# Shifting the preparation of state-space weights between GpSimd, VectorE and ScalarE in a two-layer diffusion block

## The chip, the cores and the metric

One core of a Trainium2 chip runs the whole block in one launch. The metric is the device time of one execution in microseconds; of three executions of the kernel before the median is 1510.47.

## The reference, cut to what matters

Two layers share one residual stream: 512 latent tokens and 256 context tokens of width 1024. Layer 0 is windowed grouped-query attention (16 query heads of 128, a sink logit for each head), layer 1 a bidirectional S5 state space with 128 groups of 16 channels and 64 complex states each. Every branch is gated by silu(z) and followed by an output projection and a layer norm.

```python
abar = jnp.exp(lam * dt)                                  # discretise
bbar = ((abar - 1.0) / lam)[..., None] * bmat
...
bu = jnp.einsum('btgn,gpn->btgp', u_blk, bbar)            # scan
hs = linear recurrence of bu with abar
y = jnp.einsum('btgp,gnp->btgn', hs, cmat).real
...
x = layer_norm(alpha * x + gate * ((y * jax.nn.silu(z)) @ w_out[i]), ln_g[i], ln_b[i])
```

## The kernel before, in words

The sequence is cut into steps of 8 tokens, so that the S5 layer becomes matmuls with weights that depend on the parameters alone: 64 **in-state weights** (powers of abar times B, from tokens to state), 32 **out-state weights** (C times the powers 0 to 8 of abar, from state to tokens), and a lag kernel made from them on TensorE. These weights are made on the chip while layer 0 runs, because layer 0 loads TensorE heavily and GpSimd (POOL in the profile) has little else to do. They are stored in DRAM scratch and read back in layer 1.

- `gen_w` makes one in-state weight with four tensor_tensor operations of 128x512 and 128x256 (L885 to L888), all on POOL. `w_tiles` gives it its buffers: the first EW=8, made by `early` during the first head's projections, borrow the attention's buffers `pth`, `ptl` and `zs`; the rest, made by `bg` in attention steps 1 to 21 (NW=22), have a pool of their own (`gE`, `gB`, `gm`, `gW`).
- `gen_o` makes one out-state weight: three small operations (L919 to L921) and, for each of two directions, two products and a sum over nine powers (L931 to L933, 128x576). `DO`, `DP`, `DQ` send numbers 3, 7 and 11 to VectorE (DVE), all others to POOL. Its `lag` part is 16 small matmuls (L948), two ScalarE (ACT) copies and two DVE additions, queued one weight later. QA=27 out-state weights belong to the attention from step 22 on, the other 5 to the output projection of layer 0, in its first NB=3 side steps, with buffers (`go2`) that lie where the attention's (`go`) lay.
- `layer0` runs 48 attention steps (8 head pairs by 6 blocks of 128 queries): `att_s` computes scores and softmax, `att_o` transposes the probabilities, splits them into a high and a low part (`pth`, `ptl`) and multiplies with V. Projections of the next pair ("dense" pieces) are interleaved.
- `outproj0` multiplies by the output weights, block by block of 128 tokens; `norm` computes mean and rstd (the rstd by three Newton steps on 128x1 operands, L293 and L294, and L285 ahead of them), L631 normalizes, `make_h1` transposes (L1013), scales (four tiles on DVE at L1018, four on ACT at L1020) and splits the result for layer 1, whose projection (`pul`, `puc`) follows.

All matmuls are done three times with high and low parts (`mm3`, L155 to L157). Each engine works through its instructions in order. The order on every engine comes from a planner that simulates the program with its own costs; `high_priority` with a negative offset puts the weight making behind the rest. All DMAs of the weights go through the one queue of SyncE (SP).

Of the kernel before, what the change touches and what calls it, by code (L numbers as in the profile page):

```python
# [111 lines left out]
F32 = mybir.dt.float32  # L112
# [21 lines left out]
class K:  # L134
# [141 lines left out]
    def norm(self, rs, pool):  # L276
# [14 lines left out]
        for i in range(3):  # L291
            t, yn = nt[:, 2 * i:2 * i + 1], nt[:, 2 * i + 1:2 * i + 2]
            nc.vector.scalar_tensor_tensor(t, y, xe[:, i:i + 1], y, op0=ALU.mult, op1=ALU.mult)  # L293
            nc.vector.scalar_tensor_tensor(yn, t, -3.0, y, op0=ALU.add, op1=ALU.mult)  # L294
            y = yn
# [35 lines left out]
def layer0(k, bg, early, late):  # L331
# [92 lines left out]
    def att_s(p, q, kk, qb):  # L424
# [26 lines left out]
        hs = slice(2 * p, 2 * p + 2)  # L451
        if not lat:
            nc.vector.tensor_reduce(mc, Sc, axis=AX.X, op=ALU.max)
            nc.vector.scalar_tensor_tensor(nm, mc, -SCALE, k.nsink[:, hs], op0=ALU.mult, op1=ALU.min)
# [9 lines left out]
        nc.vector.tensor_add(es, es, sm)  # L464
# [175 lines left out]
DW, DO, DP, DQ = 100, 4, 100, 14  # L640
# [215 lines left out]
def w_tiles(k, pool):  # L856
# [7 lines left out]
    z = k.qp.tile([128, 2, 768], F32, name="zs", bufs=2).rearrange("p h q -> p (h q)")  # L864
    return eb + [z[:, 512 * i:512 * i + 512].rearrange("p (d r a q) -> p d r a q", d=2, r=2, a=2) for i in range(3)]


def gen_w(k, tiles, i):
# [15 lines left out]
    tt = nc.gpsimd.tensor_tensor  # L884
# [7 lines left out]
def open_o(k, pool, q0, q1, gob):  # L892
# [3 lines left out]
    k.nc.sync.dma_start(k.dd, k.a["dd"][:, 16 * q0:16 * q1])  # L896


def gen_o(k, pool, q):

    nc, a = k.nc, k.a
    n = DO if q < DQ else DP
    eng = nc.vector if q % n == n - 1 else nc.gpsimd
# [18 lines left out]
    for d in range(2):  # L922
# [3 lines left out]
        def cc(t):  # L926
            return cb[:, t, d][:, :, None].to_broadcast([128, 4, 9, 16])

        def pb(o_):
            return pp[:, d, o_:o_ + 36].rearrange("p (g k) -> p g k", g=4)[:, :, :, None].to_broadcast([128, 4, 9, 16])  # L930
        eng.tensor_tensor(o, cc(0), pb(0), op=ALU.mult)  # L931
        eng.tensor_tensor(x, cc(1), pb(36), op=ALU.mult)  # L932
        last = eng.tensor_tensor(o, o, x, op=ALU.add)  # L933
# [70 lines left out]
def make_h1(k, b, n):  # L1004
# [4 lines left out]
    for j in range(2):  # L1009
# [4 lines left out]
        for i in range(4):  # L1014
            kk = 4 * j + i
            g, c = k.h1g[:, r, kk:kk + 1], k.h1b[:, r, kk:kk + 1]
            if j == 0:
                nc.vector.tensor_scalar(hf[:, kk], t[:, i], g, c, op0=ALU.mult, op1=ALU.add)  # L1018
            else:
                nc.scalar.activation(hf[:, kk], t[:, i], AF.Identity, bias=c, scale=g)  # L1020
# [312 lines left out]
N0, NW, EW = 1, 22, 8  # L1333
QO, QN = 32, 1
QA, NB = 27, 3
# [7 lines left out]
def main(tc, a):  # L1343
# [4 lines left out]
    k.wprio = 300  # L1348
    k.nw = NW
# [8 lines left out]
    with contextlib.ExitStack() as es:  # L1358
# [16 lines left out]
        with contextlib.ExitStack() as e2:  # L1375
# [51 lines left out]
            def gens(upto, pool):  # L1427
                nonlocal nw
                while nw < upto:
                    with tc.high_priority(offset=-GP):  # L1430
                        gen_w(k, w_tiles(k, pool), nw)
# [158 lines left out]
```

## Time and profile before

| | |
|---|---|
| median of three executions | 1510.47 us (1504.64 to 1512.83) |
| the profiled execution | 1508.56 us, its span 1506.8 us |
| TensorE busy | 1404.2 us (93%) |
| VectorE busy | 1040.2 us (69%) |
| ScalarE busy | 645.8 us (43%) |
| GpSimd busy | 635.0 us (42%) |
| mean granted TensorE clock | 0.971 of full speed |

The span runs from the first to the last instruction of the profiled execution; 1.8 us lie around it. The attention lasts from about 165 to 668 us, the output projection of layer 0 to about 870 us, layer 1 to the end. Times of rows are microseconds from the span's start.

### The profile page before, as it was taken

Reading aid. Unit: us, or ns where it says so; the run is one execution under the profiler, and the core shown is the slowest. Engines: PE = TensorE matmul, PEld = TensorE weight load, DVE = VectorE, ACT = ScalarE, POOL = GpSimd, SP = SyncE. Lnnn points to the kernel's source line nnn. Section 1 sums busy time; section 2 is a strip of 40 time slices with the busy share of each in tenths; the row PEclk is TensorE's granted clock in tenths of the full one; section 3 lists DMA queues with packets and bytes.
Section 4 is the critical chain, followed back from the end, with each engine's and each line's share of the span. In section 5 each row is a group of like instructions: output and inputs, shape, how many; then the busy total and the mean of one; then the engine's idle time right before and its main releaser. Section 6 shows DMA issues by size and latency. Waiting matters only on the chain.

```text
span 1506.8 us, 25662 instructions
## 1 busy us (share of the span) xinstructions
PE 1404.2 (93%) x9092; PEld 1134.5 (75%) x9092; DVE 1040.2 (69%) x2711; ACT 645.8 (43%) x1256; POOL 635.0 (42%) x542
## 2 busy tenths in 40 slices
PE   7999999999997899987988799999999999999997
PEld 2554789988886788875766688888777777888886
DVE  7734748777684477876759922789887896565376
ACT  1310546555464446552333234445556545343220
POOL 0004469999998676988975800000000000000240
PEclk9999999999998899998999899999999999999999
DMA  9876566766664446488795476667666796655541
GB/s 335 274 232 203 163 192 202 225 214 208 200 221 152 131 146 200 141 248 265 214 280 158 137 257 226 210 210 231 220 226 220 223 292 213 197 195 168 180 152 60
DMA packets 252639, 309.57 MB, mean 205 GB/s; under 512 B 45408, under 2 KB 151648, under 8 KB 252512
## 3 DMA queue, kind: packets, MB, share of 16 engines
q1 hardware_dynamic: 227168, 295.36, 61.5%
q10 hardware_dynamic: 25344, 12.59, 2.9%
q8 instruction: 71, 1.16, 0.3%
q14 instruction: 56, 0.46, 0.1%
HBM read 239.20 MB, written 77.07 MB: 210 GB/s over the span
## 4 chain that ended last, share of the span: by engine, by line
PE 54%; POOL 13%; DVE 13%; DMA 10%; issue 5%; ACT 3%; SPq 1%; POOLq 0%; DVEq 0%; ACTq 0%
PE pg L155 4%; PE pg L157 4%; PE pg L156 4%; PE adaps L166 3%; PE po L156 3%; PE po L157 3%; PE po L155 3%; DMA wsc<-gW 3%; PE ins L1084 3%; POOL gm L885 3%; POOL gm L886 2%; PE pul L155 2%; PE pul L156 2%; PE pul L157 2%; POOL gW L888 2%
## 5 line engine op out<-in xcount | busy, mean ns | idle before, releaser
L1318 POOL TENSOR_TENSOR xt<-xt,lng 128x512 f32<-128x512 f32 (+1 forms) x9 | 13.7, 1532 | 584.5 <-DMA xt<-n0sc 584.5
L146 DVE TENSOR_TENSOR wl<-wr,wh 128x1024 fp32r<-128x1024 f32 x104 | 137.8, 1325 | 142.9 <-ACT wh L145 140.3
L145 ACT ACTIVATE wh<-wr 128x1024 fp32r<-128x1024 f32 x104 | 109.9, 1057 | 188.0 <-PE pc L156 52.0
L155 PE MATMUL pg<-ga,wh 128*128 128x512 f32 x256 | 100.3, 392 | 0.8 <-ACT ga L1243 0.8
L157 PE MATMUL pg<-ga,wl 128*128 128x512 f32 x256 | 100.5, 393 | 0.0
L933 POOL TENSOR_TENSOR gO<-gO,gX 128x576 f32<-128x576 f32 x58 | 94.9, 1635 | 4.4
L885 POOL TENSOR_TENSOR gm<-gB,gE 128x512 f32<-128x512 f32 x56 | 78.6, 1403 | 23.6 <-DVE zs L500 19.3
L931 POOL TENSOR_TENSOR gO<-gcb,gpp 128x576 f32<-128x576 f32 x58 | 77.0, 1333 | 25.2 <-PE lag L948 20.6
L932 POOL TENSOR_TENSOR gX<-gcb,gpp 128x576 f32<-128x576 f32 x58 | 82.1, 1415 | 2.8
L886 POOL TENSOR_TENSOR gm<-gB,gE 128x512 f32<-128x512 f32 x56 | 82.6, 1475 | 0.0
L461 ACT ACTIVATE P<-P,nm 128x512 f32<-128x512 f32 (+1 forms) x64 | 49.7, 776 | 76.3 <-DVE nm L445 76.2
L487 DVE TENSOR_TENSOR ptl<-PT,pth 128x512 fp32r<-128x512 f32 (+1 forms) x96 | 60.9, 639 | 22.6 <-ACT pth L486 21.9
L1107 DVE TENSOR_TENSOR x<-m 128x64 f32<-128x64 f32 x376 | 74.7, 217 | 2.4
L146 DVE TENSOR_TENSOR gl<-gr,gh 128x512 fp32r<-128x512 f32 x48 | 50.2, 1047 | 31.2 <-ACT gh L145 31.2
L467 ACT ACTIVATE P<-P,es 128x512 f32<-128x512 f32 (+2 forms) x96 | 60.5, 682 | 19.7 <-DVE es L465 19.6
L155 PE MATMUL pq<-hh,wh 128*128 128x512 f32 x160 | 66.0, 413 | 2.8 <-ACT hh L255 2.8
L486 ACT ACTIVATE pth<-PT 128x512 fp32r<-128x512 f32 (+1 forms) x96 | 52.4, 559 | 34.4 <-PE PT L483 26.0
L483 PE MATMUL PT<-ident,P 128*128 128x128 f32 x352 | 61.3, 282 | 6.2 <-DVE vl L388 2.8
L155 PE MATMUL po<-woh,gh 128*128 128x512 f32 (+1 forms) x156 | 59.9, 394 | 7.5 <-ACT woh L580 4.7
L156 PE MATMUL pq<-hl,wh 128*128 128x512 f32 x160 | 65.8, 412 | 0.8 <-DVE hl L256 0.8
L157 PE MATMUL pq<-hh,wl 128*128 128x512 f32 x160 | 64.9, 406 | 0.3 <-DVE wl L146 0.3
L156 PE MATMUL po<-wol,gh 128*128 128x512 f32 (+1 forms) x156 | 61.7, 395 | 3.5 <-DVE wol L581 3.5
(317 smaller groups left out, 4673.2 us busy)
## 6 DMA issues: line engine op xcount, KB each, us to landing
wr<-w SPq DMA_DIRECT2D x40, 512.0 KB
osc<-gO SPq DMA_DIRECT2D x64, 256.0 KB
wr<-wout SPq DMA_DIRECT2D x32, 512.0 KB
W<-wsc SPq DMA_DIRECT2D x32, 512.0 KB
om<-osc SPq DMA_DIRECT2D x64, 256.0 KB
wr<-glu SPq DMA_DIRECT2D x32, 512.0 KB
gE<-esc SPq DMA_DIRECT2D x56, 256.0 KB
gB<-bt SPq DMA_DIRECT2D x56, 256.0 KB
```

Of the source, the lines that this page charges most:

```text
L145: nc.scalar.activation(hi, raw, AF.Copy)
L146: nc.vector.tensor_sub(lo, raw, f32(hi))
L155: mm(out, wh, mh, start=start, stop=False)
L156: mm(out, wh, ml, start=False, stop=False)
L157: mm(out, wl, mh, start=False, stop=stop)
L483: nc.tensor.transpose(T[:, j, h, :], P[h][:, c * 128:(c + 1) * 128], k.ident)
L885: tt(x(m1), x(B), eb(0), op=ALU.mult)
L886: tt(x(m2), x(B), eb(1), op=ALU.mult)
L931: eng.tensor_tensor(o, cc(0), pb(0), op=ALU.mult)
L932: eng.tensor_tensor(x, cc(1), pb(36), op=ALU.mult)
L933: last = eng.tensor_tensor(o, o, x, op=ALU.add)
L1107: nc.vector.tensor_add(x, m[:, :, 0], m[:, :, 1])
```

## The change

- `norm`: the six Newton operations become tensor_scalar with two per-partition scalars in place of scalar_tensor_tensor. In `att_s` the 128x2 operations `nm` (context blocks only) and `es` become two 128x1 tensor_scalar operations each.
- In-state weights: 12 in place of 8 are made early, the odd ones on DVE, with two fixed `zs` tiles that are used in turn; the rest are made in attention steps 1 to 19 (NW=20).
- Out-state weights: all on POOL; power 0 is a scaled copy on ACT (`k.sg`, a new small DMA at each opening), so that L931 to L933 work on 8 powers (128x512). 22 in place of 27 belong to the attention, from step 20 on, and 10 to five side steps of the output projection.
- `make_h1`: all eight scaled tiles on ACT.

```diff
-            nc.vector.scalar_tensor_tensor(t, y, xe[:, i:i + 1], y, op0=ALU.mult, op1=ALU.mult)
-            nc.vector.scalar_tensor_tensor(yn, t, -3.0, y, op0=ALU.add, op1=ALU.mult)
+            nc.vector.tensor_scalar(t, y, xe[:, i:i + 1], y, op0=ALU.mult, op1=ALU.mult)
+            nc.vector.tensor_scalar(yn, t, -3.0, y, op0=ALU.add, op1=ALU.mult)
...
-            nc.vector.scalar_tensor_tensor(nm, mc, -SCALE, k.nsink[:, hs], op0=ALU.mult, op1=ALU.min)
+            for h in range(2):
+                nc.vector.tensor_scalar(nm[:, h:h + 1], mc[:, h:h + 1], -SCALE, k.nsink[:, 2 * p + h:2 * p + h + 1],
+                                        op0=ALU.mult, op1=ALU.min)
...
-        nc.vector.tensor_add(es, es, sm)
+        for h in range(2):
+            nc.vector.tensor_scalar(es[:, h:h + 1], es[:, h:h + 1], sm[:, h:h + 1], None, op0=ALU.add)
...
+    if i < 2:
+        k.wz[i] = k.qp.tile([128, 2, 768], F32, name="zs", bufs=2).rearrange("p h q -> p (h q)")
+    z = k.wz[i % 2]
...
-    tt = nc.gpsimd.tensor_tensor
+    tt = eng.tensor_tensor
...
+    sg = pool.tile([128, 2], F32, name="sg")
+    k.nc.sync.dma_start(sg, k.a["sgn"])
+    k.sg = sg[:, 0:1]
...
-    n = DO if q < DQ else DP
-    eng = nc.vector if q % n == n - 1 else nc.gpsimd
+    eng = nc.gpsimd
...
-        eng.tensor_tensor(o, cc(0), pb(0), op=ALU.mult)
-        eng.tensor_tensor(x, cc(1), pb(36), op=ALU.mult)
-        last = eng.tensor_tensor(o, o, x, op=ALU.add)
+
+        nc.scalar.activation(o[:, :, 8 * d], cb[:, 0, d], AF.Copy, scale=k.sg)
+        o8, x8 = o[:, :, 1 - d:9 - d], x[:, :, 0:8]
+        eng.tensor_tensor(o8, cc(0), pb(0), op=ALU.mult)
+        eng.tensor_tensor(x8, cc(1), pb(36), op=ALU.mult)
+        last = eng.tensor_tensor(o8, o8, x8, op=ALU.add)
...
-            if j == 0:
-                nc.vector.tensor_scalar(hf[:, kk], t[:, i], g, c, op0=ALU.mult, op1=ALU.add)
-            else:
-                nc.scalar.activation(hf[:, kk], t[:, i], AF.Identity, bias=c, scale=g)
+            nc.scalar.activation(hf[:, kk], t[:, i], AF.Identity, bias=c, scale=g)
...
-N0, NW, EW = 1, 22, 8
+N0, NW, EW = 1, 20, 12
 QO, QN = 32, 1
-QA, NB = 27, 3
+QA, NB = 22, 5
...
-                        gen_w(k, w_tiles(k, pool), nw)
+                        gen_w(k, w_tiles(k, pool, nw), nw, nc.vector if pool is None and nw % 2 else nc.gpsimd)
```

## Rows read from the trace of the kernel before

**Rows 1.** The page: busy time, share of the span, instructions.
```profile
PE 1404.2 (93%) x9092; PEld 1134.5 (75%) x9092; DVE 1040.2 (69%) x2711; ACT 645.8 (43%) x1256; POOL 635.0 (42%) x542
```
**Rows 2.** Stretches: length, busy time by engine, clock, DMA share, GB/s.
```profile
470.00:510.00 40.00, 24.71 (x169) 21.37 (x168) 17.06 (x49) 15.10 (x36) 27.96 (x27) 0.81 0.50 156
800.00:870.00 70.00, 53.05 (x357) 45.34 (x359) 68.62 (x138) 22.09 (x47) 55.99 (x45) 0.88 0.45 144
```
**Rows 3.** Waits of TensorE from 420 to 560 us.
```profile
PE lag L948 <- POOL gO L933: 8.7, 1, 8.7
PE S L155 <- DVE nm L445: 5.8, 1, 5.8
```
**Rows 4.** Timeline of VectorE, 500 to 512 us.
```profile
503.42 0.29 DVE L919 TENSOR_TENSOR gX<-gcb,gpp 128x128 f32<-128x128 f32 x1 [6.26 <-POOL gO L933]
...
505.90 0.08 DVE L445 DVE_READ_ACCUMULATOR2_ANT nm<- 128x1 f32 x1
```
**Rows 5.** Timeline of TensorE, the matmul that follows.
```profile
506.04 0.58 PE L155 MATMUL S<-kh,qh 128*128 128x256 f32 x1 [5.77 <-DVE nm L445]
```
**Rows 6.** Timeline of GpSimd, first instructions of weights, last of one.
```profile
111.01 1.29 POOL L885 TENSOR_TENSOR zs<-ptl,pth 128x512 f32<-128x512 f32 x1 [71.14 <-DMA pth<-esc]
...
174.22 1.29 POOL L885 TENSOR_TENSOR zs<-ptl,pth 128x512 f32<-128x512 f32 x1 [10.88 <-DMA wsc<-zs]
...
201.29 1.29 POOL L885 TENSOR_TENSOR gm<-gB,gE 128x512 f32<-128x512 f32 x1 [19.32 <-DVE zs L500]
...
474.41 0.40 POOL L919 TENSOR_TENSOR gX<-gcb,gpp 128x128 f32<-128x128 f32 x1 [5.42 <-DMA gpp<-ppsc]
...
779.89 1.75 POOL L933 TENSOR_TENSOR gO<-gO,gX 128x576 f32<-128x576 f32 x1
805.58 0.87 POOL L919 TENSOR_TENSOR gX<-gcb,gpp 128x128 f32<-128x128 f32 x1 [23.93 <-DVE nt L294]
...
865.37 2.46 POOL L933 TENSOR_TENSOR gO<-gO,gX 128x576 f32<-128x576 f32 x1
```
**Rows 7.** Groups of GpSimd by form, whole span.
```profile
L933 POOL TENSOR_TENSOR gO<-gO,gX 128x576 f32<-128x576 f32 x58 | 94.9, 1635 | 4.4
...
L932 POOL TENSOR_TENSOR gX<-gcb,gpp 128x576 f32<-128x576 f32 x58 | 82.1, 1415 | 2.8
...
L931 POOL TENSOR_TENSOR gO<-gcb,gpp 128x576 f32<-128x576 f32 x58 | 77.0, 1333 | 25.2 <-PE lag L948 20.6 <-PE h1t L1013 4.4
```
**Rows 8.** Waits of GpSimd: total, times, longest.
```profile
POOL zs L885 <- DMA wsc<-zs: 35.5, 3, 18.0
...
POOL gO L931 <- PE lag L948: 20.6, 9, 9.8
POOL gX L919 <- DVE gO L933: 19.5, 3, 10.4
```
**Rows 9.** Groups of VectorE by form, 795 to 870 us.
```profile
L631 DVE TENSOR_SCALAR nrm<-R,mv,nt 128x512 f32<-128x512 f32 x11 | 10.4, 971 | 0.1
...
L1018 DVE TENSOR_SCALAR h1f<-h1t,h1g,h1b 128x128 f32<-128x128 f32 x24 | 8.2, 396 | 0.0
...
L293 DVE SCALAR_TENSOR_TENSOR nt<-nt,xe 128x1 f32<-128x1 f32 x12 | 6.3, 530 | 0.1
...
L294 DVE SCALAR_TENSOR_TENSOR nt<-nt 128x1 f32<-128x1 f32 x12 | 4.7, 390 | 0.1
```
**Rows 10.** The same lines on VectorE, 1440 to 1507 us.
```profile
L293 DVE SCALAR_TENSOR_TENSOR nt<-nt,xe 128x1 f32<-128x1 f32 x8 | 1.7, 218 | 0.2
...
L294 DVE SCALAR_TENSOR_TENSOR nt<-nt 128x1 f32<-128x1 f32 x8 | 1.3, 158 | 0.2
```
**Rows 11.** Line 288: duration in ns min/median/max, first and last start.
```profile
L288 DVE TENSOR_SCALAR ih<-ih x10: 97/153/155, 800.6 to 1500.7; 128x1 int32<-128x1 int32 x10
```
**Rows 12.** Waits of TensorE from 800 to 900 us.
```profile
PE h1t L1013 <- DVE nrm L631: 13.8, 5, 5.8
```
**Rows 13.** A group of ScalarE by form, 795 to 870 us.
```profile
L1020 ACT ACTIVATE h1f<-h1t,h1b,h1g 128x128 f32<-128x128 f32 x24 | 9.1, 457 | 32.9 <-PE h1t L1013 25.5 <-DVE H1L L1024 4.7 <-PE po L157 2.7
```
**Rows 14.** A group of VectorE by form, 160 to 668 us.
```profile
L464 DVE TENSOR_TENSOR es<-es,sm 128x2 f32<-128x2 f32 x48 | 22.6, 470 | 13.4 <-ACT es L463 13.0 <-ACT P L461 0.2
```

More of the change, by code (lines that the diff above doesn't have):

```diff
@@ L450, in att_s @@
             scores(h, Sc[:, h], C, 384, nw)
-        hs = slice(2 * p, 2 * p + 2)
         if not lat:
             nc.vector.tensor_reduce(mc, Sc, axis=AX.X, op=ALU.max)
-            nc.vector.scalar_tensor_tensor(nm, mc, -SCALE, k.nsink[:, hs], op0=ALU.mult, op1=ALU.min)
+            for h in range(2):
+                nc.vector.tensor_scalar(nm[:, h:h + 1], mc[:, h:h + 1], -SCALE, k.nsink[:, 2 * p + h:2 * p + h + 1],
+                                        op0=ALU.mult, op1=ALU.min)
         for h in range(2 if lat else 0):
@@ L637, in outproj0 @@
         out_half(k, 0, half, order[half], gsrc, k.wop, body(half), side)
-DW, DO, DP, DQ = 100, 4, 100, 14
 MAGIC = 12582912.0
@@ L853, in powers, with w_tiles @@
         yield
-def w_tiles(k, pool):
+def w_tiles(k, pool, i):
     sh = [128, 2, 2, 2, 64]
@@ L863, in w_tiles, with gen_w @@
           for n in ("pth", "ptl")]
-    z = k.qp.tile([128, 2, 768], F32, name="zs", bufs=2).rearrange("p h q -> p (h q)")
-    return eb + [z[:, 512 * i:512 * i + 512].rearrange("p (d r a q) -> p d r a q", d=2, r=2, a=2) for i in range(3)]
-def gen_w(k, tiles, i):
+    if i < 2:
+        k.wz[i] = k.qp.tile([128, 2, 768], F32, name="zs", bufs=2).rearrange("p h q -> p (h q)")
+    z = k.wz[i % 2]
+    return eb + [z[:, 512 * j:512 * j + 512].rearrange("p (d r a q) -> p d r a q", d=2, r=2, a=2) for j in range(3)]
+def gen_w(k, tiles, i, eng):
     nc, a = k.nc, k.a
@@ L926, in cc @@
         def cc(t):
-            return cb[:, t, d][:, :, None].to_broadcast([128, 4, 9, 16])
+            return cb[:, t, d][:, :, None].to_broadcast([128, 4, 8, 16])
         def pb(o_):
-            return pp[:, d, o_:o_ + 36].rearrange("p (g k) -> p g k", g=4)[:, :, :, None].to_broadcast([128, 4, 9, 16])
-        eng.tensor_tensor(o, cc(0), pb(0), op=ALU.mult)
-        eng.tensor_tensor(x, cc(1), pb(36), op=ALU.mult)
-        last = eng.tensor_tensor(o, o, x, op=ALU.add)
+            return pp[:, d, o_:o_ + 36].rearrange("p (g k) -> p g k", g=4)[:, :, 1 - d:9 - d][:, :, :, None].to_broadcast([128, 4, 8, 16])
+        nc.scalar.activation(o[:, :, 8 * d], cb[:, 0, d], AF.Copy, scale=k.sg)
[3 more added lines that the diff above has]
+        last = eng.tensor_tensor(o8, o8, x8, op=ALU.add)
         O.append(o)
@@ L1348, in main @@
     k.wprio = 300
+    k.wz = {}
     k.nw = NW
```

## The prediction

> **What bounds the kernel now.** I read the page first: TensorE is busy 1404.2 of 1506.8 us [rows 1]. Its matmuls stay the same, so the change can only move the 102.6 us in which it idles, and what a lowered clock costs beside that. Next the busy time by stretch. Two stretches stand out before layer 1 [rows 2]: 470 to 510 us, where TensorE idles 15.3 of 40 us at a granted clock of 0.81, and 800 to 870 us, where it idles 17.0 of 70 us at 0.88. In the second VectorE is busy 68.6 of 70 us: there VectorE is the bound. Then the waits. In the first stretch they are two single ones: 8.7 us for GpSimd's first out-state weight and 5.8 us for the row maximum `nm` on VectorE [rows 3]. In the second, the transposes wait 13.8 us for the normalized rows [rows 12].
>
> The timeline of VectorE shows where the 5.8 us come from. At 503.42 it starts out-state weight 3, for which it had stood 6.26 us in its queue because GpSimd still held the buffer `gX`; `nm` stood behind that and was done at 505.98, and the score matmul that needed its buffer started at 506.04 after 5.77 us of idling [rows 4, 5]. So one of the three weights on VectorE costs TensorE directly.
>
> GpSimd's timeline [rows 6] gives the schedule of the weights: early in-state weights in four pairs from 111.01, the last pair from 174.22; the other 56 from 201.29 to about 469 (474.41 less its wait of 5.4), 4.8 us each; out-state weights from 474.41 to 781.6, that is 113 us past the end of the attention at 668; a hole of 23.9 us; the last five from 805.58 to 867.8, in the very stretch that VectorE bounds.
>
> **The change part by part.**
>
> *Out-state weights off VectorE.* The wait behind number 3 cannot arise. I take off the 5.8 us [rows 3, 5]. Bounds: 0, if the score matmul then waits for something else, and 6.6. The other two weights gave TensorE no such wait, and GpSimd, which waited 19.5 us for the three [rows 8], makes them itself instead.
>
> *GpSimd's work.* Going from nine powers to eight takes a ninth off three operations of 1.33, 1.42 and 1.64 us [rows 7]: 0.49 us for each direction, 0.97 for each weight, 31 us in all. An in-state weight takes 4.8 us, so the four more early ones, which partly fill the 19.3 us hole ahead of 201.29 [rows 6], end the in-state weights some 19 us sooner, near 450. The old pace of out-state weights was 307 us for 24 on GpSimd, 12.8 us each with all waits; at 11.8 us the 22 end near 450 + 8 + 260 = 718 rather than 781.6. With the same hole of 24 us the other ten run from 742 on; the last five took 12.4 us each, (867.8 - 805.6)/5, and at 11.4 us ten end near 856, against 867.8. All this is off TensorE's path but for the lags: the first lag's 8.7 us arise because the planner thinks GpSimd earlier than it is. It has 52 in place of 56 weights to fall behind in, but out-state making is also due two steps sooner; I take 3 us off (bounds 0 and 8.7).
>
> *Norm and make_h1, 800 to 870 us.* L293 and L294 take 0.530 and 0.390 us here, 0.218 and 0.158 at the kernel's end, where GpSimd works little [rows 9, 10]. They have two tensors in SBUF as inputs. The one-input tensor_scalar at L288 has the same size and lies between them, and its longest is 0.155 [rows 11]. I price the new form at 0.16. The 12 and 12 of the later Newton steps then save 12 x 0.37 + 12 x 0.23 = 7.2 us, the six and six of the first step half of that again: 10.8. The tiles of L1018 take another 8.2 us off VectorE. That is 19 of its 68.6 us. TensorE idles 17.0 us there, so that is the ceiling at this clock. ScalarE pays: eight tiles of 0.457 us in a row instead of four beside VectorE's four [rows 13], 1.8 us more latency for each of six blocks, 11 us if none hides; it is busy 22 of 70 us, and the blocks overlap. I take 10 us off; bounds 3 (19 less 11, less what the split then waits) and 17.
>
> The Trainium skill ("SBUF — State Buffer", the part on which engines share ports) says that a VectorE instruction with two SBUF inputs and a GpSimd one that reads SBUF exclude each other for their whole length, while one with a single SBUF input outside the two-port modes does not contend. Rows 9 to 11 agree with it for these lines. By the same rule an early pair on VectorE and GpSimd would run in turn rather than together, which would lengthen the term for the early weights below by perhaps 2 us.
>
> *Small operations of the attention.* `es` takes 0.470 us [rows 14]; two at 0.16 take 0.32, 7 us of VectorE over the attention. The work that hides it is that of TensorE, which rarely waits for it: I count nothing, at most 2 off.
>
> *Twelve early weights.* The four pairs are 21 us apart, (174.22 - 111.01)/3, of which the wait for the buffers' write-out is 35.5/3 = 12 us and the making 9.3 [rows 6, 8]. Half of each pair on VectorE saves up to 4.6 us of making. Six pairs then end between 190 and 224 us rather than at 182. The first attention output stands behind them, since it needs `pth`, `ptl` and `zs`, and TensorE has some two dense pieces to run meanwhile before their PSUM buffers are used up. I add 4 us; bounds 0 and 15. VectorE's six weights stand ahead of weight splits in its queue; TensorE waits for neither today.
>
> *Power 0 on ScalarE.* There are 64 copies of 128x64; the nearest row is 0.457 us for 128x128 [rows 13], so 0 to 29 us on an engine that is busy 43% of the time [rows 1]. The new thing is the wait: each copy needs a `gO` buffer that the lag matmuls of an earlier weight must release, for which GpSimd now waits 20.6 us in nine places [rows 8]. ScalarE would wait there with the softmax and the weight splits behind it. I add 1 us; bounds 0 and 20.6. The small `sg` loads are three DMAs more on SP; nothing waits for them but the copies.
>
> Sum against the profiled execution: 1508.6 - 5.8 - 3 - 10 + 4 + 1 = 1494.8. That execution lies 1.9 us under the median of the runs shown, and some of the clock comes back with fewer holes: 1494 it is.
>
> **Rivals.**
>
> *ScalarE inherits the buffer wait* and hands it to TensorE. For: 20.6 us of such waits exist, the longest 9.8. Against: the planner sees the lag that releases the buffer and places the copy behind it, and TensorE's own waits for GpSimd were only 8.7 us. Price up to 20.6: 1494 - 1 + 20.6 = 1513, no change.
>
> *The early weights hold up the attention; this one ends slower.* If pairs keep their 21 us, the sixth ends 42 us after the fourth did, at 224, and every later step shifts by what TensorE can't fill. Wholly uncovered that gives 1490 + 42 = 1532; with some 11 us of dense pieces as cover, 1521. It decides from 28 us of uncovered delay on (1490 + 28 = 1518). For: the first outputs already stand right behind the last pair. Against: pairs two to four shared SP with loads that thin out by then.
>
> *Ten weights in the output projection come too late.* If the second set starts at 806 as now, ten of 11.4 us end near 920, and the last lag stands ahead of layer 1 in TensorE's queue, which by my sum begins near 858: 1494 + 62 = 1556. It decides, at 1518, from a start 24 us after my 742. Against: the 22 weights end 64 us sooner by the sum above, and GpSimd has little else in its queue.
>
> *The narrow tensor_scalar still waits for GpSimd.* L631 is a tensor_scalar too, and takes 0.97 us for 512 elements, more than its share [rows 9]; if the narrow ones behaved so, 10.8 us of VectorE's saving would go and the third term shrink to 3: 1501. L288 speaks against it. The Trainium skill ("VectorE: DVE Perf Modes", on the mode with both read ports) lists tensor_scalar among the operations that can take both ports. No run here shows it for a 128x1 operand.
>
> **How the numbers follow.** The forecast gets 0.56, ScalarE's wait 0.16, the early weights 0.12, the late ten 0.09, the waiting tensor_scalar 0.07. A measurement here can tell about 0.5%, 7.6 us, from no change: faster is under 1502.9, slower over 1518. The forecast's own range is 1480 to 1503: below, two of the three gains at their upper bounds with the costs as they are; above, where faster ends. Faster is 0.56 and most of the 0.07, 0.61; same ScalarE's 0.16 and a little of the others, 0.20; slower the early and the late weights less that little, 0.19. The range begins at 1477, where the gains stand at 5.8, 8.7 and 17 and the costs at nothing; its end of 1516 reaches past ScalarE's 1513 and leaves out the early and the late weights.
>
> **What would show it.** Right: no wait of TensorE for `nm` near 500 us; L293 and L294 as tensor_scalar near 0.16 us while GpSimd works; VectorE clearly under 68 of 70 us in the norm stretch; GpSimd done with its last weight near 856 us. Wrong: the first `pth` or `zs` of the attention waiting for in-state weights past 190 us with TensorE idle; ScalarE waiting for lag matmuls ahead of a copy; the last `lag` later than the first `pul`.

## The result and the profile after

The changed kernel takes 1495.95 us, the median of five executions (1494.1 to 1500.11), against 1506.45 us for the kernel before, the median of five as well. The ratio is 0.9927 with a 95% interval of [0.9903, 0.9951]; the interval lies below 1, so the kernel is faster, by 0.7%. The profiled execution took 1495.95 us with a span of 1494.0. 1494 was predicted, but the sum came out for partly other reasons, and some luck is in the hit: the prediction stood on three executions of the kernel before with a median of 1510.47, 16.5 us above it, and with five that median is 1506.45, so that 10.5 us lie between the medians. Between the two profiled executions they are 12.6 us, where the sum had 13.8.

I cut the span at three instructions of TensorE, the first output matmul `po`, the first projection matmul of layer 1 `pul` and the first `pg` in layer 1:

| | before | after | difference | of which TensorE idle | of which TensorE busy |
|---|---|---|---|---|---|
| start to first `po` (attention) | 669.0 | 677.6 | +8.6 | +7.1 | +1.5 |
| `po` to `pul` (the output stretch) | 201.6 | 183.8 | -17.8 | -9.6 | -8.2 |
| `pul` to `pg` (layer 1, first part) | 324.0 | 319.1 | -4.9 | -1.2 | -3.8 |
| `pg` to the end | 312.2 | 313.5 | +1.3 | +1.4 | 0.0 |

The attention, which was to become 3.8 us shorter, is longer. All of the gain is behind it. And TensorE's idle time, which the prediction set out to shorten, is hardly shorter in all: 100.3 us after 102.6. The other 10.5 us are busy time, although the matmuls are the same (the profile models the ends of matmuls, so that busy time is an estimate). Most of that is in the output stretch (length, then busy time of PE, PEld, DVE, ACT, POOL, then granted clock, DMA share, GB/s; before, then after):

```profile
669.00:871.00 202.00, 170.04 (x963) 134.94 (x962) 155.42 (x234) 62.08 (x116) 161.50 (x125) 0.91 0.69 212
677.00:862.00 185.00, 162.58 (x936) 131.10 (x936) 135.76 (x211) 76.06 (x167) 128.29 (x109) 0.95 0.78 238
```

TensorE idles 9.5 us less there, and the granted clock is 0.95 of full speed in place of 0.91. With 170.0 x 0.91 / 0.95 = 162.9 the clock alone accounts for about the difference in busy time; some of it may also belong to the 27 matmul records that the stretch has fewer. The page of after has the same matmuls, and less work on VectorE and GpSimd, more on ScalarE, as in [rows 1]:

```profile
PE 1393.7 (93%) x9092; PEld 1126.4 (75%) x9092; DVE 1011.5 (68%) x2748; ACT 669.5 (45%) x1344; POOL 605.2 (41%) x545
```

Busy time by stretch shows where TensorE lost time in the attention. First before:

```profile
160.00:240.00 80.00, 74.02 (x514) 65.71 (x514) 49.79 (x145) 42.37 (x99) 47.86 (x47) 0.98 0.65 189
400.00:480.00 80.00, 74.42 (x475) 66.94 (x473) 55.30 (x120) 47.82 (x116) 70.98 (x64) 0.98 0.59 193
480.00:560.00 80.00, 66.40 (x470) 56.69 (x471) 43.97 (x94) 32.30 (x84) 55.74 (x52) 0.89 0.45 136
```

And after, the same stretches:

```profile
160.00:240.00 80.00, 66.89 (x440) 57.18 (x440) 48.43 (x155) 38.44 (x87) 35.16 (x33) 0.96 0.61 174
400.00:480.00 80.00, 60.74 (x366) 53.46 (x366) 50.48 (x97) 37.29 (x93) 71.97 (x65) 0.89 0.60 189
480.00:560.00 80.00, 78.00 (x580) 68.40 (x579) 48.84 (x114) 45.65 (x125) 68.74 (x70) 0.98 0.45 140
```

The hole of [rows 2] near 490 us is gone (11.6 us), but TensorE idles 13.7 us more from 400 to 480 and 7.1 more from 160 to 240. The waits of TensorE from 420 to 560 name the new hole; the two waits of [rows 3], 14.5 us, are not among them any more:

```profile
PE O L155 <- ACT pth L488: 17.0, 4, 15.2
PE O L156 <- DVE ptl L489: 1.7, 1, 1.7
```

Three timelines tell why ScalarE was late with `pth`. SyncE's queue first (start, duration), then ScalarE, then TensorE:

```profile
463.94 0.32 SPq L893 DMA_DIRECT2D wsc<-gW  x1
...
464.79 0.44 SPq L902 DMA_DIRECT2D sg<-sgn  x1
465.28 0.42 SPq L911 DMA_DIRECT2D gcb<-cb  x1
```

```profile
451.39 0.28 ACT L464 ACTIVATE es<-nm,sink 128x1 f32<-128x1 f32 x1
468.33 0.59 ACT L938 ACTIVATE gO<-gcb,sg 128x64 f32<-128x64 f32 x2 [16.66 <-issue]
```

```profile
470.54 0.58 PE L155 MATMUL O<-pth,vh 128*128 128x256 f32 x1 [15.19 <-ACT pth L488]
```

From about 451.7 on ScalarE does nothing: next in its queue stands the first power-0 copy (L938). Its inputs `sg` and `gcb` are loaded into the buffers of the out-state weights, which lie where those of the in-state weights lay, and the loads are issued at 464.79 and 465.28, behind the write-out of the last in-state weight at 463.94. Softmax and `pth` stand behind the copy. The row of the copy names no releaser (`issue`); asked for the tile `sg`, the trace lists the copy as waiting 16.7 us for it. That the copy makes the hole is shown by the first experiment below. In that hole the granted clock falls as well: 0.72 of full speed (between the two levels) as the mean of 450 to 480 us, with TensorE busy 13.1 of 30.

The stretch that VectorE bounded before, now from 790 to 861 us, answers to the second line of [rows 2]:

```profile
790.00:861.00 71.00, 59.94 (x409) 50.38 (x409) 61.83 (x130) 35.31 (x85) 41.95 (x37) 0.98 0.70 215
```

VectorE no longer fills it, and the waits of TensorE for the transposes there, 13.8 us in [rows 12], are down to 5.5. The longest wait is now the one for GpSimd's weights; over the whole output stretch it is 10.5 us, against 1.1 before:

```profile
PE lag L957 <- POOL gO L942: 6.4, 3, 3.9
PE h1t L1022 <- ACT h1f L1026: 4.8, 3, 2.8
PE h1t L1022 <- DVE nrm L633: 0.7, 1, 0.7
```

GpSimd's last operation of the last weight starts at 832.10, where [rows 6] had 865.37:

```profile
832.10 1.27 POOL L942 TENSOR_TENSOR gO<-gO,gX 128x512 f32<-128x512 f32 x1
```

### The profile page after: what moved, and what is told of

Same layout as the page of the kernel before. It is cut to its first block, busy times and chain, and to the rows that moved or that the text cites. A ratio compares the mean times of both kernels' runs of the same rounds, so it can differ in the third digit from the quotient of the medians.

```text
span 1494.0 us, 25811 instructions
## 1 busy us (share of the span) xinstructions
PE 1393.7 (93%) x9092; PEld 1126.4 (75%) x9092; DVE 1011.5 (68%) x2748; ACT 669.5 (45%) x1344; POOL 605.2 (41%) x545
## 4 chain that ended last, share of the span: by engine, by line
PE 56%; DVE 14%; DMA 13%; POOL 6%; ACT 6%; issue 5%; SPq 1%; ACTq 0%; POOLq 0%; DVEq 0%
DMA wr<-wout 4%; PE pg L155 4%; PE pg L157 4%; PE pg L156 4%; PE ins L1090 3%; PE adaps L166 3%; DMA wsc<-gW 3%; PE pul L155 2%; PE pul L156 2%; ACT X L1133 2%; PE pul L157 2%; PE PT L485 2%; PE pq L156 2%; DVE wl L146 2%; DMA gr<-gsc 2%
## 5 line engine op out<-in xcount | busy, mean ns | idle before, releaser
L155 PE MATMUL pg<-ga,wh 128*128 128x512 f32 x256 | 100.3, 392 | 0.3 <-ACT ga L1249 0.3
L942 POOL TENSOR_TENSOR gO<-gO,gX 128x512 f32<-128x512 f32 x64 | 95.5, 1492 | 4.5
L889 POOL TENSOR_TENSOR gm<-gB,gE 128x512 f32<-128x512 f32 x52 | 74.5, 1432 | 32.6 <-ACT wh L145 28.6
L940 POOL TENSOR_TENSOR gO<-gcb,gpp 128x512 f32<-128x512 f32 x64 | 78.6, 1235 | 13.1 <-issue 5.9
L941 POOL TENSOR_TENSOR gX<-gcb,gpp 128x512 f32<-128x512 f32 x64 | 81.6, 1274 | 3.4
L489 DVE TENSOR_TENSOR ptl<-PT,pth 128x512 fp32r<-128x512 f32 (+1 forms) x96 | 60.8, 638 | 23.6 <-ACT pth L488 23.3
L890 POOL TENSOR_TENSOR gm<-gB,gE 128x512 f32<-128x512 f32 x52 | 75.9, 1459 | 0.0
L155 PE MATMUL O<-pth,vh 128*128 128x256 f32 x176 | 53.0, 301 | 22.1 <-ACT pth L488 19.4
L469 ACT ACTIVATE P<-P,es 128x512 f32<-128x512 f32 (+2 forms) x96 | 60.6, 681 | 18.2 <-DVE es L467 17.8
```

The costliest lines, as they stand in the source:

```text
L155: mm(out, wh, mh, start=start, stop=False)
L889: tt(x(m1), x(B), eb(0), op=ALU.mult)
L890: tt(x(m2), x(B), eb(1), op=ALU.mult)
L940: eng.tensor_tensor(o8, cc(0), pb(0), op=ALU.mult)
L941: eng.tensor_tensor(x8, cc(1), pb(36), op=ALU.mult)
L942: last = eng.tensor_tensor(o8, o8, x8, op=ALU.add)
```

## The experiments

Theory A: the gain comes from taking VectorE out of the attention's and the norm's way, and is cut by two holes that the change makes itself, ScalarE's and that of the early weights. The rival, theory B: GpSimd's chain of weights sets the end of the output stretch, so that a hole of TensorE in the attention costs little and what counts is when GpSimd is done. The table holds all kernels that ran, one profile each. "GpSimd left" is the time from the first `po` to the end of the last weight.

| kernel | ratio to before | attention | GpSimd left | output stretch | `pul` to `pg` |
|---|---|---|---|---|---|
| before | 1 | 669.0 | 198.8 | 201.6 | 324.0 |
| after | 0.9927 [0.9903, 0.9951] | 677.6 | 155.8 | 183.8 | 319.1 |
| e1_first_two_nine | 0.9926 [0.9902, 0.995] | 671.8 | 161.6 | 185.6 | 322.5 |
| e7_nine_all | 0.9943 [0.9919, 0.9968] | 666.1 | 185.9 | 195.6 | 317.4 |
| e2_early8_pool | 0.9868 [0.9821, 0.9916] | 663.2 | 177.2 | 190.9 | 317.1 |
| e3_early12_pool | 0.9912 [0.989, 0.9934] | 680.3 | 144.4 | 182.2 | 320.2 |
| e8_both | 0.9878 [0.9837, 0.9918] | 660.3 | 182.5 | 196.4 | 320.4 |
| e4_norm_only | 0.9979 [0.9951, 1.0008] | 670.1 | 193.7 | 194.8 | 319.9 |
| e14_norm_undone | 0.9967 [0.995, 0.9984] | 679.9 | 158.6 | 191.1 | 322.2 |
| e13_wide_es_nm | 1.0001 [0.9982, 1.002] | 681.3 | 155.5 | 187.4 | 322.8 |
| e10_no_dve_o | 1.0067 [1.0044, 1.0091] | 662.7 | 220.8 | 221.9 | 319.1 |
| e12_dve_o_back | 0.9966 [0.9948, 0.9984] | 676.4 | 159.1 | 189.2 | 323.6 |
| e9_27_5 | 0.9955 [0.993, 0.9981] | 675.6 | 172.5 | 194.0 | 317.6 |
| e15_planned_later | 1.015 [1.0125, 1.0176] | 648.2 | 243.8 | 244.9 | 321.2 |

Each profile is one execution, while the executions of a kernel spread over up to 16 us (e4). The profiled one lies up to 4.4 us below the median of its kernel (e7, and 3.8 for e4) and up to 3.5 above it (e14). Differences of a few microseconds between two rows are therefore no more than a hint.

### ScalarE's hole

**e1_first_two_nine**: in the first two out-state weights of after GpSimd makes all nine powers.

```diff
-        nc.scalar.activation(o[:, :, 8 * d], cb[:, 0, d], AF.Copy, scale=k.sg)
+        if q < 2:
+            eng.tensor_tensor(o, c9[0], p9[0], op=ALU.mult)
+            eng.tensor_tensor(x, c9[1], p9[1], op=ALU.mult)
+            last = eng.tensor_tensor(o, o, x, op=ALU.add)
+        else:
+            nc.scalar.activation(o[:, :, 8 * d], cb[:, 0, d], AF.Copy, scale=k.sg)
...
```

> The changed kernel, but the first two out-state weights are made with all nine powers on GpSimd, so that ScalarE's queue holds no copy that waits for the first load after the buffers change hands. Theory A (the 16.7 us in which ScalarE stood at a copy is what emptied TensorE from 455 to 470 us): the hole goes, TensorE idles under 10 us between 440 and 490, and the kernel runs 10 to 17 us faster than the changed one, some 1480 to 1486, ratio to before 0.982 to 0.986. Rival B (GpSimd's first out-state weight is late in any case, and TensorE would wait for the first lag matmul as it did before): a wait for GpSimd of 8 us or more appears in the same place and the gain is under 5 us, ratio 0.989 to 0.993.

The hole goes: TensorE is busy 35.9 of the 40 us from 440 to 480 (after: 23.1), and the attention ends 5.8 us sooner, much less than the 15.2 of the hole. In its place TensorE waits for the first weight on GpSimd:

```profile
440.00:480.00 40.00, 35.93 (x222) 32.04 (x220) 28.57 (x55) 24.24 (x61) 33.45 (x31) 0.91 0.52 173
```

```profile
PE lag L964 <- POOL gO L943: 5.2, 1, 5.2
```

The cause of the hole is thereby shown, and yet the total stays the same, 0.9926, which is in the range of B: the stretch got 1.8 us longer and layer 1 3.4. About half of the latter is TensorE's busy time, at a granted clock of 0.91 in place of 1.00 in the first 20 us of layer 1.

**e7_nine_all**: the same for all 32 weights, so that no copy is left on ScalarE (`if True` in place of `if q < 2`).

> The changed kernel, but all out-state weights with nine powers on GpSimd, no copies on ScalarE at all. Theory A (only the first copies hurt): about as the kernel with the first two changed, less what GpSimd's 31 us more work costs; the last out-state weights end some 20 us later, near 850, and TensorE waits for lag matmuls; ratio 0.984 to 0.990. Rival B (GpSimd's ninth is what the change gains by): ratio 0.992 or above.

The attention ends 11.5 us sooner than in after, the stretch is 11.8 us longer, and the ratio 0.9943, in the range of B; the intervals overlap. The copies give back in the output stretch about what they cost in the attention. It is not the waits for GpSimd's weights that grow there (9.5 us, after 10.5) but those for the normalized rows, from 0.7 to 8.3.

### The early weights

**e2_early8_pool**: eight early in-state weights as before, all on GpSimd, everything else as in after.

```diff
-N0, NW, EW = 1, 20, 12
+N0, NW, EW = 1, 20, 8
...
-  gen_w(k, w_tiles(k, pool, nw), nw, nc.vector if pool is None and nw % 2 else nc.gpsimd)
+  gen_w(k, w_tiles(k, pool, nw), nw, nc.gpsimd)
```

> The changed kernel, but 8 early in-state weights, all on GpSimd, as before; 56 remain for the steps 1 to 19. Theory A (the two more pairs hold pth, ptl and zs and cost TensorE some 8 us from 160 to 190 us): TensorE idles under 4 us there instead of 10, and GpSimd ends the in-state weights near 469 again. If nothing else follows, 4 to 8 us faster than the changed kernel; the in-state weights end later than in it by up to 5 us, which may lengthen ScalarE's wait for the first load by as much. Ratio to before 0.987 to 0.993. Rival B (the early stall is made by VectorE's share, not by the number): TensorE's idling there stays above 8 us only if the number matters little; then the ratio is 0.992 to 0.996.

This kernel has the lowest median, 1488.11 us of four executions. From 160 to 200 us TensorE is busy 37.8 of 40 us, first e2, then after:

```profile
160.00:200.00 40.00, 37.82 (x285) 32.90 (x284) 27.70 (x103) 24.58 (x60) 6.33 (x7) 1.00 0.51 132
```

```profile
160.00:200.00 40.00, 29.57 (x215) 24.57 (x215) 27.46 (x99) 18.77 (x42) 12.30 (x12) 0.96 0.53 154
```

The four additional weights cost TensorE 8.3 us there. In the total e2 is 14.4 us ahead at the end of the attention and loses 7.1 in the output stretch. GpSimd is done 7.0 us later, but TensorE does not wait longer for its weights there (8.6 us, after 10.5); that the one makes the other is not shown.

**e3_early12_pool** leaves the twelve, but makes all on GpSimd (the second pair of lines above alone).

> The changed kernel with its 12 early in-state weights all on GpSimd. Theory A (the number counts: six pairs hold the buffers that the attention's first outputs need, and VectorE's half shortens each pair): each pair is made 4 us slower, the last ends near 205 rather than 187, TensorE idles 20 us or more from 160 to 220 instead of 13; ratio to before 0.995 to 1.003. Rival B (VectorE's half is what stalls the start, since softmax and splits stand behind the weights in its queue): TensorE idles less than 10 us there, ratio 0.986 to 0.990.

It stays with after (0.9912, between the ranges of the two theories), and TensorE has 27.9 of 40 us from 160 to 200. So it is the number of early weights that costs, and VectorE's half of them hardly matters. Waits of ScalarE from 150 to 215 us in e3 show a part of the mechanism, `pth` held by a weight that borrows its buffer; TensorE waits 7.0 us for `pth` there:

```profile
ACT pth L488 <- POOL zs L890: 5.0, 2, 4.2
```

**e8_both** has the edits of e1 and e2.

> The changed kernel with 8 early in-state weights on GpSimd and the first two out-state weights with nine powers on GpSimd, that is the two experiments before in one. Theory A, as it stands after them (the early weights cost 8 us; behind ScalarE's wait at the first copies stands GpSimd itself, so that freeing ScalarE alone gains little): ratio to before 0.983 to 0.988, no more than 5 us below the kernel with 8 early weights alone, and a wait of TensorE for the first lag matmul of 5 to 12 us near 490. Rival B (the two holes are independent, and what the first experiment gained in the attention was lost later by chance of the order): the attention ends some 6 us sooner than with 8 early weights alone and the ratio is 0.979 to 0.983.

The gains don't add: the attention ends another 2.9 us sooner than in e2, the stretch is 5.5 us longer, the ratio 0.9878. TensorE now waits 12.3 us for the first lag, so that with ScalarE out of the way GpSimd is what it meets, as theory A has it.

### Norm and make_h1

**e4_norm_only**: the kernel before with the two Newton lines as tensor_scalar and all eight tiles of `make_h1` on ScalarE.

```diff
-            nc.vector.scalar_tensor_tensor(t, y, xe[:, i:i + 1], y, op0=ALU.mult, op1=ALU.mult)
+            nc.vector.tensor_scalar(t, y, xe[:, i:i + 1], y, op0=ALU.mult, op1=ALU.mult)
...
-            if j == 0:
-                nc.vector.tensor_scalar(hf[:, kk], t[:, i], g, c, op0=ALU.mult, op1=ALU.add)
-            else:
-                nc.scalar.activation(hf[:, kk], t[:, i], AF.Identity, bias=c, scale=g)
+            nc.scalar.activation(hf[:, kk], t[:, i], AF.Identity, bias=c, scale=g)
```

> The kernel before with two edits alone: the Newton steps as tensor_scalar, and all eight tiles of make_h1 on ScalarE. Theory A (the norm stretch is bound by VectorE and these two edits free it): VectorE's busy time from 800 us to the first projection of layer 1 falls by some 15 us, the stretch shortens by 7 to 12 us, ratio to before 0.992 to 0.995. Rival B (most of the 18 us that the changed kernel gained between 668 and 861 us comes from the out-state weights, which no longer stand in the tail): under 4 us, ratio 0.997 to 1.0.

The output stretch is 6.8 us shorter than before, at a ratio of 0.9979 that alone can't be told from 1. In the 800 to 870 us of [rows 2] VectorE's 68.6 us fall to 58.5, but TensorE gains little of it. Where it waited 1.1 us for GpSimd's weights, it now waits 9.4 us in the output stretch, 5.4 of them for the last one, just ahead of layer 1:

```profile
800.00:870.00 70.00, 53.86 (x378) 45.71 (x377) 58.47 (x114) 32.56 (x78) 56.16 (x45) 0.90 0.49 154
```

```profile
PE lag L948 <- POOL gO L933: 9.4, 3, 5.4
```

**e14_norm_undone** is the other way round, after with these lines as they were before.

> The changed kernel with the norm's Newton steps as scalar_tensor_tensor and half of make_h1's tiles on VectorE again. Theory A (these two edits are worth 7 to 10 us in the norm stretch, as the prediction's third term has it): the stretch from the first output matmul to layer 1 grows from 184 to about 191 to 194 us, ratio to before 0.997 to 1.000. Rival B (with the weights out of the tail GpSimd is done 34 us before the stretch ends, VectorE is held up less, and the two edits are worth little): growth under 4 us, ratio 0.993 to 0.996.

The stretch is 7.3 us longer than in after; the ratio 0.9967 is 0.4% above it, and the intervals just overlap. Both directions give about 7 us for the stretch, in single profiles; by the ratios the two edits are worth some 3 us in the kernel before and 6 in after, neither clear of the noise. In e4 the stretch gains almost what theory A has and the ratio is in the range of B; in e14 the stretch is in the range of A and the ratio lies between the two.

### The small operations of the attention

**e13_wide_es_nm**: after with `nm` and `es` as one operation for both heads, as before.

```diff
-            for h in range(2):
-                nc.vector.tensor_scalar(nm[:, h:h + 1], mc[:, h:h + 1], -SCALE, k.nsink[:, 2 * p + h:2 * p + h + 1],
-                                        op0=ALU.mult, op1=ALU.min)
+            nc.vector.scalar_tensor_tensor(nm, mc, -SCALE, k.nsink[:, 2 * p:2 * p + 2], op0=ALU.mult, op1=ALU.min)
...
-        for h in range(2):
-            nc.vector.tensor_scalar(es[:, h:h + 1], es[:, h:h + 1], sm[:, h:h + 1], None, op0=ALU.add)
+        nc.vector.tensor_add(es, es, sm)
```

> The changed kernel with the attention's es and nm as one 128x2 operation each again. Theory A (TensorE's work hides them): VectorE is busy some 7 to 12 us more over the attention, the ratio stays within 0.002 of the changed kernel's 0.993. Rival B (they stand in the softmax's path and free it): 0.996 or above.

The whole measured gain is gone: 1.0001, in the range of B. The groups of VectorE from 160 to 680 us, after first, then e13 (busy time, mean ns of one):

```profile
L466 DVE TENSOR_SCALAR es<-es,sm 128x1 f32<-128x1 f32 x96 | 19.9, 209 | 46.7 <-ACT es L464 27.5 <-ACT P L462 18.9
...
L454 DVE TENSOR_SCALAR nm<-mx,nsink 128x1 f32<-128x1 f32 x32 | 5.4, 203 | 0.1
```

```profile
L463 DVE TENSOR_TENSOR es<-es,sm 128x2 f32<-128x2 f32 x48 | 25.1, 524 | 28.6 <-ACT es L462 23.5 <-ACT P L460 4.4
...
L453 DVE SCALAR_TENSOR_TENSOR nm<-mx,nsink 128x2 f32<-128x2 f32 x16 | 6.5, 404 | 0.1
```

That is 25.3 against 31.6 us, 6.3 less of VectorE over the attention, and it can't by itself make the 11.3 us that lie between the two spans. These sit 3.7 us in the attention, 3.6 in the output stretch and 3.7 in the first part of layer 1; in the last two neither operation occurs. In layer 1 3.0 of the 3.7 are TensorE's busy time, at a granted clock of 0.85 in the first 20 us where after has 1.00. The waits of TensorE in e13 from 160 to 680 us have another order of things, a hole near 460 that now ends with `P`, and small waits that after has shorter (`ptl` 3.8 us, `cf` 1.0):

```profile
PE PT L482 <- ACT P L466: 12.2, 3, 11.5
PE O L156 <- DVE ptl L486: 5.3, 5, 1.8
PE trp L804 <- DVE cf L836: 5.2, 2, 4.2
```

How much of the 0.7% the operations cost and how much the other order that the planner made of them is not settled, and with it whether they stand in the softmax's path, as B has it; I had no run that holds the order and changes the operations alone.

### Out-state weights and VectorE

**e10_no_dve_o**: the kernel before with its three VectorE weights on GpSimd, nothing else.

```diff
-DW, DO, DP, DQ = 100, 4, 100, 14
+DW, DO, DP, DQ = 100, 100, 100, 14
```

> The kernel before with all out-state weights on GpSimd, nothing else changed. Theory A (the wait for nm at 500 us comes from the weight on VectorE): the 5.8 us wait is gone; GpSimd makes three more weights, 33 us, less the 19.5 us in which it waited for VectorE, so that the 27 end some 13 us later, near 795; the ratio is 0.996 to 0.999. Rival B (TensorE then waits for GpSimd's weights instead): waits for lag matmuls of 6 us or more between 490 and 600 and a ratio of 0.999 to 1.004.

The attention ends 6.3 us sooner, and the kernel is still 0.67% slower, more than either theory allowed. GpSimd makes three weights more, and they come out at the end: the last is done at 883.5 in place of 867.8. TensorE's waits from 662 to 885 us:

```profile
PE lag L948 <- POOL gO L933: 15.7, 3, 8.2
PE po L155 <- ACT woh L580: 11.2, 1, 11.2
```

**e12_dve_o_back** gives weights 3, 7 and 11 back to VectorE in after.

```diff
-    eng = nc.gpsimd
+    eng = nc.vector if q in (3, 7, 11) else nc.gpsimd
```

> The changed kernel with out-state weights 3, 7 and 11 on VectorE again. Theory A (a weight on VectorE stalls the scores behind it, and the changed kernel's GpSimd has time to spare at its end): a wait of TensorE for nm or mx of 4 us or more behind one of the three; the last weight ends 10 to 20 us before 833; no gain in the tail; ratio 0.994 to 0.998. Rival B (GpSimd's time is what counts, as when the three were taken off VectorE in the kernel before, which cost 0.7%): ratio 0.986 to 0.991.

Slower than after by 0.4% (the intervals just overlap), but by another way than theory A, whose range the ratio is in: no wait of TensorE for `nm` near 500 comes back. GpSimd waits for VectorE's weights and wins nothing by the help; its last weight is done at 835.5, not 10 to 20 us before 833:

```profile
POOL gX L925 <- DVE gO L942: 29.9, 3, 10.4
```

### The split of the weights, and the bound behind it

**e9_27_5**: after with 27 out-state weights in the attention and 5 in the output projection.

```diff
-QA, NB = 22, 5
+QA, NB = 27, 3
```

> The changed kernel with 27 out-state weights in the attention and 5 in the output projection, as before (three side steps). Theory A (GpSimd works through the weights one after the other, wherever they are counted, and only the hole of 24 us at the change of buffers moves): the last weight ends within 10 us of the changed kernel's 833, the output projection takes the same 184 us within 4, ratio 0.989 to 0.996. Rival B (the gain of the output projection comes from the shift of weights): the stretch from the first output matmul to the first projection of layer 1 grows to 192 us or more, ratio 0.997 or above.

The stretch is 10.2 us longer than in after, as theory B has it, with GpSimd done 14.8 us later; the ratio 0.9955 is still in the range of A. Yet TensorE's waits for GpSimd's weights in the stretch are under 1 us here: the shift of the weights costs, but hardly by waits for them.

**e15_planned_later**: e8 with the first out-state weight tied in the planner's order, without a wait on the chip, behind the scores of step 35, and the 22 weights spread from there to step 47.

```diff
-    eng.tensor_tensor(by, cb[:, 2], qb(72), op=ALU.mult)
+    m = eng.tensor_tensor(by, cb[:, 2], qb(72), op=ALU.mult)
+    if q == 0:
+        k.tc.add_manual_dep(ins_of(m), ins_of(k.last_s).name,
+            mybir.DependencyInfo(mybir.DependencyClass.NoSync, mybir.DependencyReason.DATA), reason="plan")
...
-                    out_q(min(QA, (n - NW + 1) * QA // (47 - NW)), n == 47)
+                    out_q(min(QA, max(0, (n - 35 + 1) * QA // (48 - 35))), n == 47)
```

> The kernel with 8 early weights and the first two out-state weights with nine powers on GpSimd, and in it the first out-state weight tied, in the planner's order alone and not by a semaphore, behind the scores of attention step 35, with the 22 weights spread from there; the first lag matmuls stand some 60 instructions further back in TensorE's queue. Theory A (the hole near 480 us is there because the planner puts the first out-state work where it thinks GpSimd has got to, ahead of where GpSimd is): TensorE's wait of 12.3 us for the first lag falls below 4 us; GpSimd, which does not wait for the planner, ends its last weight within 10 us of the 843 of the kernel it is made from; ratio to before 0.979 to 0.986. Rival B (the time is lost again where the lags, now closer together, or the tail stand): the attention ends within 3 us of the 660 of the kernel it is made from, or the output projection takes 5 us more, ratio 0.986 to 0.991.

`k.last_s` is the last score matmul queued. Theory A fails here, and the ratio is above the range of B as well. TensorE's hole is gone, 36.1 of 40 us busy from 480 to 520 (e8: 23.9), and the attention ends at 648.2, the earliest of all. But GpSimd now idles, at one place 21.5 us for a lag matmul that the new order has set back and that must release its buffer, and the kernel is the slowest of all, 1.015:

```profile
520.00:560.00 40.00, 40.00 (x277) 35.39 (x277) 25.03 (x63) 24.67 (x59) 13.97 (x14) 1.00 0.27 88
```

```profile
POOL gbb L930 <- PE lag L967: 21.5, 1, 21.5
```

```profile
PE lag L967 <- POOL gO L952: 56.1, 10, 10.5
```

The last row is from the waits of TensorE between 648 and 894 us. The last weight is done at 892.0; layer 1 begins 1.1 us later. Theory B fits wherever GpSimd has much left: in before, e4, e10 and e15 the stretch lasts 1.1 to 2.8 us longer than GpSimd. In e4, e10 and e15 TensorE's last wait there is indeed for GpSimd's last weight (5.4, 7.0 and 6.4 us). In before it is not: GpSimd ends just as late, but TensorE's longest waits are those for the normalized rows. Where GpSimd has 144 to 186 us left, the stretch no longer follows it one for one, 182 to 196 us, and other things bound it. A version that removes the hole of TensorE and keeps GpSimd busy was not found.

## Why the prediction came out, point by point

**"All this is off TensorE's path but for the lags" failed.** The prediction had GpSimd's weights 12 us sooner done and counted nothing for it. They are done 34 us sooner (833.4, predicted 856), and GpSimd was a second bound of the output stretch before, close behind VectorE: it had 198.8 us left in 201.6, and TensorE waits for it as soon as VectorE alone is relieved (e4). That is a term that was missing. Undoing the split alone costs 10.2 us of the stretch (e9), undoing eight powers 11.8 (e7). By which way is shown only in part. About half of these losses is TensorE's busy time (5.3 and 5.8 us, at a granted clock of 0.92 and 0.94, after 0.95), and its waits for GpSimd's weights do not grow in either. The pace of the weights was taken too slow: the first 22 need 232.4 us (468.51 to 700.95, where GpSimd's wait of 23.6 before 724.56 begins), 10.6 each, not 11.8, and the other ten 10.9. The start was taken too early, 450 against 463.9 for the end of the in-state weights: the pace of 4.8 us is right, but the first of the 52 starts at 214.88, 13.6 us later than in before. The hole between, predicted with 24 us, is 23.6.

**What a lowered clock costs was left out of the sum**, but for the 0.8 us between 1494.8 and 1494. Of the 12.8 us between the two spans 10.5 are busy time of the same matmuls, and only 2.3 are idling. In the output stretch the idling fell by 9.6 us, about the 10 that were predicted; the 8.2 us of busy time are what the stretch gained beyond them. How much of this one execution's clock belongs to the kernel is open: the mean granted clock is 0.971 and 0.977 in the two profiles, 0.974 to 0.977 in the five executions of after and 0.968 to 0.976 in 25 of before.

**Norm and make_h1, predicted -10**: right in its mechanism, about 7 of the stretch in size (e4 and e14). The price of the narrow operation was off: 0.267 and 0.206 us, not 0.16. Groups of VectorE in after, 670 to 833 us, with GpSimd at work, and 834 to 861, behind its last weight:

```profile
L633 DVE TENSOR_SCALAR nrm<-R,mv,nt 128x512 f32<-128x512 f32 x5 | 5.0, 1027 | 0.0
...
L293 DVE TENSOR_SCALAR nt<-nt,xe 128x1 f32<-128x1 f32 x6 | 1.6, 262 | 0.0
L294 DVE TENSOR_SCALAR nt<-nt 128x1 f32<-128x1 f32 x6 | 1.2, 197 | 0.0
```

```profile
L633 DVE TENSOR_SCALAR nrm<-R,mv,nt 128x512 f32<-128x512 f32 x6 | 3.1, 541 | 0.1
L293 DVE TENSOR_SCALAR nt<-nt,xe 128x1 f32<-128x1 f32 x6 | 1.6, 272 | 0.1
L294 DVE TENSOR_SCALAR nt<-nt 128x1 f32<-128x1 f32 x6 | 1.3, 215 | 0.2
```

L293 and L294 are no shorter with GpSimd idle, so the rival in which the narrow form still waits for GpSimd is out. L288, from which the price came, has two constants as scalars (0.14 us), L294 one constant and one per-partition operand, L293 two of these: the rows go up with the operands read, some 0.06 us each. I took the price from an instruction of the same size, not of the same operands. At the kernel's end the old form took 0.218 and 0.158 us [rows 10] and the new one takes 0.272 and 0.211: alone the new form is the longer one, and it gains only beside GpSimd. The Newton operations save 8.7 us (12 x 0.263 + 12 x 0.184 + 6 x 0.321 + 6 x 0.241, from the rows of after against those of before), not 10.8.

The Trainium skill ("SBUF — State Buffer", the section "SBUF: two separate sides") says that VectorE with two SBUF inputs and a GpSimd instruction that reads SBUF hold a pair of ports against each other for whole instructions. The traces agree: L293 in its old form took 0.530 us beside GpSimd and 0.218 at the kernel's end [rows 9, 10], and the form with one input shows no gain from GpSimd's end in the two fences above (0.262 and 0.272 us).

GpSimd's share in this is visible in L633, a tensor_scalar over 512 elements: 1.027 us beside GpSimd in after and 0.541 behind its last weight. By kernel the means are 0.971 us in before [rows 9] and 1.001 in e4, with GpSimd busy 56 of 70 us; 0.762 in after, with 42 of 71; 0.703 in e14, with 34 of 70. So a part of VectorE's relief there comes from GpSimd's earlier end, not from the edits of `norm`. The Trainium skill ("VectorE: DVE Perf Modes", the section on the perf-mode tiers) lists tensor_scalar with a mode that uses both read ports; the rows of L633 go with that (1.027 and 0.541 us), those of the 128x1 operations do not (0.262 and 0.272).

**Weights off VectorE, predicted -5.8**: right in place and size where it was looked for (e10: the attention 6.3 us shorter, no wait for `nm` near 500 in after). Not seen was that this edit alone moves three weights to the end of GpSimd's chain, and makes the kernel slower, 1.0067. The rival with the late weights has the right mechanism: in after it is paid for by eight powers and by the earlier start. "First lag, -3" came to 8.7 off, as its wait is gone; but only because ScalarE's hole now comes first. e1 brings 5.2 of it back.

**Power 0 on ScalarE, predicted +1**: this step failed in size and in cause. I looked for a wait on the lag matmuls of an earlier weight; the wait is on the first load behind the change of buffers (of `sg` there are two, not three). It stops the in-order queue of ScalarE for 16.7 us and TensorE for 15.2, within the bound of 20.6 that was drawn for another reason; ScalarE's waits for lag matmuls ahead of a copy come to 3.8 us in four places. That freeing ScalarE (e1) shortens the attention by only 5.8 us goes with theory B: the planner starts the out-state weights earlier than GpSimd gets to them, and TensorE meets GpSimd's delay at the next lag, 5.2 us in e1 and 12.3 in e8. Of the 5.8 us 4.0 are left at the first `pul`. Why the total shows none of them is settled only for the 1.7 us of busy time in layer 1.

**Twelve early weights, predicted +4**: 8.3 us of TensorE, inside the bounds of 0 and 15, twice the value taken. The sixth pair ends at 190 us, the near end of the 190 to 224 that I gave it, and it still costs: the attention of these steps waits in small pieces (`pth`, `nm`, `mx`), and GpSimd itself idles 28.6 us before the first weight of its own pool. e2 without them has the lower median.

**Small operations, counted nothing**: the 7 us of VectorE were meant for `es` alone, from 0.470 to 0.32 us each. It takes 0.418 (2 x 0.209), which saves 2.7 us over the attention against before; that `es` and `nm` together come to 6.3 is luck. That TensorE's work hides the saving is not borne out: undoing the two costs 0.7% (e13). This is the largest single miss against a prediction of at most 2 us, and its mechanism is open.

**The first part of layer 1**, where nothing is edited, gives 4.9 of the 12.8 us between the two spans. The 14 kernels have 317.1 to 324.0 us there with no order by their edits that I can see. In the first 20 us of it the granted clock is 0.92 before and 1.00 after, which is a part of it: the five kernels with 1.00 there take 317.1 to 320.2 us, the nine with 0.85 to 0.95 take 319.1 to 324.0. The rest is not explained, and differences of that size between two profiles should not be read as effects of an edit.

So the time was hit by errors of both signs: the attention 12 us worse than the sum had it, the output stretch 8 better, layer 1 3.6 better by something not forecast. That these nearly cancel is luck.

## What to carry to other kernels

When work is taken from an engine "off the path", compare when its whole chain ends with when the next stage begins: GpSimd was 3 us ahead of the end of the output stretch, so that three more weights made the kernel slower although a wait of TensorE vanished. Before a small operation is put on an in-order engine that also feeds the critical one, ask for its first instance, not the average one: at a change of buffers its load waits for the last write-out, and everything queued behind waits too. Price a small instruction from one with the same kinds of operands, and try each part of a bundle without the others: without the additional early weights this one gives 1.3% instead of 0.7% (four executions, and the two intervals overlap slightly). And compare TensorE's busy time as well as its idle time: here most of the gain stands in the former.

## What was not expected of the hardware

- A tensor_scalar of VectorE on 128x1 costs by its per-partition operands: 0.14 to 0.15 us with constants alone, 0.20 to 0.22 with one such operand, 0.25 to 0.27 with two, with GpSimd at work or idle. The scalar_tensor_tensor at the end of before has the same step, 0.158 us with a constant and 0.218 with a per-partition scalar [rows 10].
- Two 128x1 tensor_scalar instructions (2 x 0.209 us) are shorter than the one 128x2 tensor_tensor that they replace (0.470 in before, 0.524 in e13) while GpSimd works; no run shows the pair without GpSimd.
